# A two-layer decoder trunk on one core: the gate products of the S5 mixer in float32

## The chip, the cores and the metric

The kernel runs on one core of a Trainium2 chip. The time is that of the device for one execution, in microseconds; several executions of the same kernel are taken and the median is given. The engines are named as in the profile: PE (TensorE, matrix products), PEld (its weight loads), DVE (VectorE), ACT (ScalarE), POOL (GpSimd) and SP (SyncE, here only a queue that issues transfers).

## The reference

```python
h = x                                               # (1, 256, 1024), float32
for layer in range(2):
    h = h + 0.5 * swiglu(rms_norm(h), w_gate, w_up, w_down)       # width 2816
    hn = rms_norm(h)
    h = h + (s5_mixer(hn, ...) if layer == 0 else moba_mixer(hn, ...))
    h = h + 0.5 * swiglu(rms_norm(h), w_gate, w_up, w_down)

def s5_mixer(h, w_in, ..., d_skip, w_glu, w_out):
    u = h @ w_in                                    # 256 x 1024
    # 64 groups of 16 channels, 64 complex states each:
    #   state = lambda * state + B u;   y = Re(C state) + d_skip * u
    g = gelu(y)
    g = g * sigmoid(g @ w_glu)                      # the gate, 1024 x 1024
    return g @ w_out
```

All arrays are float32.

## The kernel before, in words

The six stages run one after the other: f00 (the first SwiGLU), s5, f01, f10, moba, f11. All order on the engines is written out by hand: the program's order is each engine's order, and no scheduler changes it.

**Split products.** A float32 matrix is taken apart into a high part, rounded to fewer bits (the type fp32r in the profile), and a low part, the difference. A product is then three: high by high, high by low, low by high, added up in PSUM. `Stream` does this for the weights. A unit is 256 rows (or two times 128 by 512) of a weight, 1 MB, loaded from HBM into one of three raw buffers in the order of the list `units`; a raw buffer is loaded again when its unit has been freed. `split` makes the high part of half a unit on ACT (L84, or L90 where a gain is multiplied in) and the low part on DVE (L85, L91) and puts both in one of nine slots; after the second half the unit is free. `pump` splits the next half in the list if it has been loaded and a slot is free, and does nothing otherwise; `get` splits until the wanted half is there; `release` gives a slot back. So a call of `pump` splits whatever comes next in the list, ahead of its use.

**S5.** Four input products (`w_in`, lines L397 to L399, two column halves by two row halves) give U, by way of ACT (L976) and a transposition on DVE (L977). The state is computed in eight blocks b of 128 channels, with tables that were prepared during f00, went to HBM and come back as TA, TE and TB, three buffers each:

- `t1(b)`: the scan input on PE (L986), from TA and U, into a PSUM bank. Blocks 0 to 3 need the first column half of U, blocks 4 to 7 the second.
- `rot(b)`: on DVE a rotation and two scans (L1005 to L1011), with decays rh from ACT (L995); on POOL the rotation back (L1015 to L1018), which gives hr. `t1rot(b)` is both, `t1ld` and `rot_ld` are the two with the next loads.
- `y_out(b)`: the output on PE (L1044), from TB, U and hr; gelu on ACT (L1048); a transposition by 32 on DVE into gs (L1051).
- `g_tr(b)`: two transposes on PE (L1060); the result goes as high part (L1062, ACT), low part (L1063, DVE) and in float32 (L1064, ACT, into gf) to SBUF.
- `glu(b)`: the gate products of the block (L1077 to L1079), eight output tiles by three products of 256 columns, into four PSUM banks.

The loop runs `y_out(b)`, `glu(b - 3)`, `t1rot(b + 3)`, `g_tr(b - 1)`. Four times `gate` follows: a sigmoid on ACT, the product with gf on DVE, and its high and low part, both on DVE (L1092, L1093). Then come the output products `so` (L397 to L399) in four blocks; the last two are done in `boundary` together with the entry of f01.

**The front.** While the first weights arrive, `busy` lets PE multiply ones; `quarter` transposes a quarter of x and multiplies the gain in (L1339 on ACT, L1340 on DVE); the first products are L471. `tables` is a generator that prepares the S5 tables during f00, a step at a time: `fill`, called beside the products, advances it by one yield. Its scalar part runs on POOL (L686 to L692), with one reciprocal on DVE (L774).

Of the kernel before, what the change touches and what calls it, by code (L numbers as in the profile page):

```python
# [10 lines left out]
F32 = mybir.dt.float32  # L11
F32R = mybir.dt.float32r
AF = mybir.ActivationFunctionType
OP = mybir.AluOpType
# [11 lines left out]
TWO_PI = 2.0 * math.pi  # L26
MAGIC = 12582912.0

XO = {'f00': 124, 's5': 124, 'g': 8, 'f01': 80, 'f10': 8, 'moba': 124, 'f11': 8}
AO = (68, 68, 68, 68)  # L30
OO = 68

# [3 lines left out]
class Stream:  # L36


    def __init__(self, nc, units, raw_pool, hl_pool):
        self.nc, self.units, self.rp, self.hp = nc, units, raw_pool, hl_pool  # L40
        self.raw = {}
        self.issued = {}
        self.clock = lambda: 0.0
        self.aged = True
        self.freed = set()
        self.nd = 0
        self.halves = []
        self.first = {}
        for u in range(len(units)):
            self.first[u] = len(self.halves)  # L50
            self.halves += [(u, 0), (u, 1)]
        self.hl = {}
        self.slots = list(range(HB - 1))
        self.ns = 0
        self.dmas()
# [63 lines left out]
def trunk_kernel(ctx: ExitStack, tc, x, ffn_norm, ffn_w_gate, ffn_w_up, ffn_w_down, mix_norm,  # L119
# [3 lines left out]
    nc = tc.nc  # L123
# [4 lines left out]
    xp = ctx.enter_context(tc.tile_pool(name="xt", bufs=1))  # L128
# [5 lines left out]
    def psM():  # L134
        return pp.tile([128, 512], F32, name="pM", tag="M", bufs=2)

    def psR():
        return pp.tile([128, 512], F32, name="pR", tag="R", bufs=2)

    def psA(i):  # L140
        return pp.tile([128, 512], F32, name=f"pA{i}", tag=f"A{i}", bufs=1)

    mm = nc.tensor.matmul


    NB = 8
# [6 lines left out]
    units = []  # L153
    where = {}
    GAIN = {"f00": None, "f01": 8, "f10": 16, "f11": 24, "s5": 32, "moba": 40}

    def add(key, load, gains=None):

        where[key] = len(units)
        units.append((key, load, gains))  # L160

    ahead = []

# [13 lines left out]
    def ld_rows(w, r0):  # L177
        def f(t):
            nc.sync.dma_start(t.rearrange("p (k c) -> p k c", c=1024),
                              w[r0:r0 + 256, :].rearrange("(k p) c -> p k c", p=128))  # L180
        return f
# [16 lines left out]
    def s5_units():  # L198
        for nh in range(2):
            for a in range(2):  # L200
                add(("win", nh, a), ld_cols(s5_w_in[0], a * 512, nh * 512), GAIN["s5"] + 4 * a)
        for b in range(4):
            add(("glu", b), ld_rows(s5_w_glu[0], b * 256))
        for b in range(4):
            add(("so", b), ld_rows(s5_w_out[0], b * 256))

    QKV = [("k", 0), ("q", 0), ("k", 1), ("q", 1), ("v", 0), ("v", 1)]
    QOFF = {"q": 0, "k": 1024, "v": 2048}
# [106 lines left out]
    def home(pool, ph):  # L315

        xa = pool.tile([128, 4224], F32R, name="xa")
        v = xa[:, XO[ph]:XO[ph] + 4096].rearrange("p (i k c) -> p i k c", i=2, c=256)
        return v[:, 0], v[:, 1]
# [298 lines left out]
    def tables(tp):  # L618
# [3 lines left out]
        def T(name, *shape):  # L622
            return tp.tile([128] + list(shape), F32, name=name)
# [147 lines left out]
            pt(lt[:, 1, :, o], u2[:, 1], w2[:, 0], OP.add)  # L771

        cfr, cfi = T("cfr", 32), T("cfi", 32)
        V.reciprocal(rden, den)  # L774
        pts(y, lr, -1.0, OP.add)
        pt(e0, y, ar, OP.mult)
# [180 lines left out]

    def s5(nxt, entry):
        V, P = nc.vector, nc.gpsimd
        HALVES = (slice(0, 64), slice(64, 128))  # L960
        wstack = ExitStack()
        wp = wstack.enter_context(tc.tile_pool(name="s5", bufs=1))
# [8 lines left out]
        def w_in(nh, t, hooks, pumps=(1, 5)):  # L971
            uA, uB = where["win", nh, 0], where["win", nh, 1]
            ps = psM()
            product(ps, t, uA, uB, hooks, pumps)
            us = wp.tile([128, 512], F32, name="us", bufs=1)
            nc.scalar.activation(us, ps, AF.Identity, scale=Rr[t])  # L976
            V.transpose(U[:, nh * 16:(nh + 1) * 16, t, :], us.rearrange("p (q c) -> p q c", c=32))  # L977

        def t1(b):
            tv = TA.pop(b).rearrange("p (i q c) -> p i q c", i=2, c=128)  # L980
            ps = psA(b) if b < 4 else psM()
            for i in range(2):
                for q in range(4):
                    c = i * 256 + q * 64
                    for r in HALVES:
                        mm(ps[r, c:c + 64], tv[:, i, q, r], U[:, 4 * b + q, :, :], start=True, stop=True)  # L986
            S[b] = ps
# [33 lines left out]
        def t1ld(b):  # L1021
            t1(b)
            if b + 3 < NB:
                ld_a(b + 3)

        def t1rot(b):
            t1ld(b)
            rot_ld(b)

        def rot_ld(b):  # L1030
            rot(b)
            if 0 < b < NB - 2:
                ld_e(b + 2)

        def y_out(b):
            tb = TB.pop(b)
            v2 = tb[:, 0:1024].rearrange("p (i q c) -> p i q c", i=2, c=128)
            v3 = tb[:, 1024:1536].rearrange("p (q c) -> p q c", c=128)
            ps = psR()
            hr = H.pop(b)  # L1040
            for q in range(4):
                for i, (v, z) in enumerate(((v3[:, q], U[:, 4 * b + q]), (v2[:, 0, q], hr[:, 0, q]), (v2[:, 1, q], hr[:, 1, q]))):
                    for r in HALVES:
                        mm(ps[r, q * 64:(q + 1) * 64], v[:, r], z, start=i == 0, stop=i == 2)  # L1044
            if b + 3 < NB:
                ld_b(b + 3)
            yg = wp.tile([128, 4, 2, 32], F32, name="yg", bufs=1)
            nc.scalar.activation(yg.rearrange("p q t c -> p (q t c)"), ps[:, 0:256], AF.Gelu_apprx_tanh)  # L1048
            gs = wp.tile([128, 2, 4, 32], F32, name="gs", bufs=2)
            for t in range(2):  # L1050
                V.transpose(gs[:, t], yg[:, :, t, :])  # L1051
            GS[b] = gs

        def g_tr(b):
            ps = psR()
            gs = GS.pop(b)
            if b == 0:
                GT["h"], GT["l"] = home(xp, "g")
            for t in range(2):
                nc.tensor.transpose(ps[:, t * 128:(t + 1) * 128], gs[:, t].rearrange("p q c -> p (q c)"),  # L1060
                                    ident)
            nc.scalar.activation(GT["h"][:, b, :], ps[:, 0:256], AF.Copy)  # L1062
            V.tensor_tensor(GT["l"][:, b, :], ps[:, 0:256], GT["h"][:, b, :].bitcast(F32), op=OP.subtract)  # L1063
            nc.scalar.activation(gf[b // 2][:, b % 2, :], ps[:, 0:256], AF.Copy)  # L1064

        def glu(b, os=range(8)):

            u = where["glu", b // 2]
            if b == 0:
                for i in range(4):  # L1070
                    acc[i] = psA(i)
            gh, gl = GT["h"][:, b, :], GT["l"][:, b, :]
            wh, wl = st.get(u, b % 2)
            for o in os:
                d = acc[o // 2][:, (o % 2) * 256:(o % 2) * 256 + 256]
                c = slice(o * 128, o * 128 + 128)
                mm(d, wh[:, c], gh, start=b == 0 and o % 2 == 0, stop=False, skip_group_check=True)  # L1077
                mm(d, wh[:, c], gl, start=False, stop=False, skip_group_check=True)
                mm(d, wl[:, c], gh, start=False, stop=b == NB - 1, skip_group_check=True)  # L1079
                if o == 7:  # L1080
                    st.release(u, b % 2)
                if o == 3 and b < 5 or o == 7 and b in (3, 4) or o == 5 and b == 4:
                    st.pump()

        def gate(i):

            sg = fp.tile([128, 2, 256], F32, name="sg", tag="gr", bufs=2)
            nc.scalar.activation(sg, acc[i].rearrange("p (a c) -> p a c", a=2), AF.Sigmoid)
            g = gf[i]
            V.tensor_tensor(g, g, sg, op=OP.mult)  # L1090
            gh, gl = (GT[p][:, 2 * i:2 * i + 2, :] for p in "hl")
            V.tensor_copy(gh, g)  # L1092
            V.tensor_tensor(gl, g, gh.bitcast(F32), op=OP.subtract)  # L1093

        def so(b, t, n, last=False):
# [6 lines left out]
        w_in(0, 0, entry_hooks("s5") if entry else {})  # L1102
        w_in(0, 1, {})
        w_in(1, 0, {3: [lambda: t1rot(0)], 5: [lambda: t1rot(1)]})
        w_in(1, 1, {1: [lambda: t1rot(2)], 4: [lambda: t1ld(3)]}, ())
        rot_ld(3)
        y_out(0)
        y_out(1)
        t1ld(4)
        g_tr(0)  # L1110
        rot_ld(4)
        y_out(2)
        g_tr(1)
        t1rot(5)
        for b in range(3, NB):
            y_out(b)
            glu(b - 3)
            if b + 3 < NB:
                t1rot(b + 3)
            g_tr(b - 1)  # L1120
        wstack.close()
        lstack.close()
        XP[0] = xstack.enter_context(tc.tile_pool(name="xt2", bufs=1))
        g_tr(7)
        st.pump(2)
        warm(AF.Sigmoid)
        glu(5)
        for i in range(4):
            glu(6, (2 * i, 2 * i + 1))
            glu(7, (2 * i, 2 * i + 1))  # L1130
# [211 lines left out]
    def busy(n):  # L1342

        ps = psR()
        for _ in range(n):
            mm(ps[:, 0:128], ones, ones, start=True, stop=True)
# [29 lines left out]
    busy(7)  # L1376
    quarter(0, gains)
    busy(3)
    st.pump()
    next(tab, None)  # L1380
    square(0, 0)
# [68 lines left out]
```

## Time and profile before

| | |
|---|---|
| median of 3 runs | 1001.4 us (1000.97 to 1001.5) |
| the profiled execution | 1001.1 us |
| its span | 999.3 us |
| PE busy | 979.9 us of it |
| DVE busy | 703.3 us |
| ACT busy | 575.7 us |
| POOL busy | 167.2 us |

The profile shows one execution. A timeline's line gives the start in us from the span's start, the length, engine, line, operation, output <- inputs, the forms, and in brackets the idle time of the engine before it with what ended it. A view of the stretches gives for each engine its busy time and its number of instructions, then the clock granted to PE as a share of full speed, the busy share of the transfer engines and GB/s. A view of the waits gives the waiting instruction, what it waited for, the sum in us, how often, and the longest. The front lies in the first 30 us, S5 from about 224 us to about 333 us.

### The profile page before, as it was taken

The page shows a single profiled execution, that of the slowest core. Times are in us where ns is not written, and L with a number is a line of the kernel's source. Part 1 is how long each engine was busy: PE and PEld are TensorE (multiplying, and loading weights), DVE is VectorE, ACT ScalarE, POOL GpSimd, SP SyncE. Part 2 cuts the span into 40 slices and gives each one's busy share as a digit, 9 for nine tenths or more (in the row PEclk, how much of TensorE's full clock was granted, in tenths as well). Part 3 has the DMA queues.
Part 4 walks back from the last instruction along what each step waited for, and adds up shares of the span by engine and source line. Part 5 has one row for each costly group of instructions (what it writes and reads, how often), then busy time and mean ns, then how long its engine had stood idle before and what let it go on. Part 6 is the DMA issues. An engine that isn't in the chain of part 4 may idle for free.

```text
span 999.3 us, 17186 instructions
## 1 busy us (share of the span) xinstructions
PE 979.9 (98%) x6700; PEld 870.9 (87%) x6700; DVE 703.3 (70%) x1147; ACT 575.7 (58%) x1045; POOL 167.2 (17%) x330
## 2 busy tenths in 40 slices
PE   8999999999889999999999999999999999999998
PEld 6778888888778999999999999998888899999997
DVE  4799676858978776666657766665689667766662
ACT  6647778744245655555455655553798656555541
POOL 4881222113740100000010000000441010000000
PEclk9999999999999999999999999999999999999999
DMA  8978776886846566555527665655354446756531
GB/s 234 275 259 257 263 250 214 277 325 217 283 139 214 179 199 219 184 192 185 189 81 227 215 209 175 206 172 171 128 169 148 154 162 212 241 180 210 170 128 42
DMA packets 138081, 198.67 MB, mean 199 GB/s; under 512 B 16320, under 2 KB 109584, under 8 KB 137744
## 3 DMA queue, kind: packets, MB, share of 16 engines
q1 hardware_dynamic: 133808, 184.32, 57.1%
q0 software_dynamic: 3616, 12.66, 3.2%
q8 instruction: 52, 0.85, 0.4%
q10 hardware_dynamic: 576, 0.61, 0.3%
q14 instruction: 29, 0.24, 0.1%
HBM read 183.89 MB, written 13.66 MB: 198 GB/s over the span
## 4 chain that ended last, share of the span: by engine, by line
PE 86%; DVE 7%; POOL 3%; issue 2%; ACT 2%; DMA 1%; SPq 0%; ACTq 0%; DVEq 0%
PE pM L552 12%; PE pM L551 12%; PE pM L553 12%; PE pA L397 9%; PE pA L399 9%; PE pA L398 9%; PE pM L397 5%; PE pM L398 5%; PE pM L399 5%; DVE wlo L85 2%; DVE zo L1011 1%; POOL sc L686 1%; PE pR L331 1%; PE pR L880 1%; ACT whi L84 1%
## 5 line engine op out<-in xcount | busy, mean ns | idle before, releaser
L551 PE MATMUL pM<-xa,whi 128*128 128x256 f32 x1056 | 295.7, 280 | 0.0
L552 PE MATMUL pM<-xa,whi 128*128 128x256 f32 x1056 | 294.9, 279 | 0.0
L553 PE MATMUL pM<-xa,wlo 128*128 128x256 f32 x1056 | 294.7, 279 | 0.0
L91 DVE SCALAR_TENSOR_TENSOR wlo<-raw,gT,whi 128x512 fp32r<-128x512 f32 x328 | 228.1, 747 | 71.2 <-ACT whi L90 71.0
L85 DVE TENSOR_TENSOR wlo<-raw,whi 128x1024 fp32r<-128x1024 f32 (+1 forms) x157 | 191.6, 1234 | 57.6 <-ACT whi L84 56.4
L90 ACT ACTIVATE whi<-raw,gT 128x512 fp32r<-128x512 f32 x328 | 213.6, 711 | 19.6 <-PE pA L399 14.7
L552 PEld LDWEIGHTS pM<-xa,whi 128*128 128x128 f32 x1056 | 198.5, 188 | 2.6
L551 PEld LDWEIGHTS pM<-xa,whi 128*128 128x128 f32 x1056 | 198.5, 188 | 2.3
L553 PEld LDWEIGHTS pM<-xa,wlo 128*128 128x128 f32 x1056 | 198.5, 188 | 0.0
L84 ACT ACTIVATE whi<-raw 128x1024 fp32r<-128x1024 f32 (+1 forms) x157 | 160.9, 1049 | 28.0 <-DMA raw<-in_ffn_w_up_dram 6.4
L397 PE MATMUL pA<-whi,ah 128*128 128x512 f32 x352 | 138.8, 394 | 0.0
L398 PE MATMUL pA<-wlo,ah 128*128 128x512 f32 x352 | 137.6, 391 | 0.0
L399 PE MATMUL pA<-whi,al 128*128 128x512 f32 x352 | 137.6, 391 | 0.0
L566 ACT ACTIVATE sg<-gr 128x256 f32<-128x256 f32 x66 | 27.6, 418 | 165.8 <-DVE gr L563 165.8
L397 PE MATMUL pM<-whi,xa 128*128 128x512 f32 x288 | 119.5, 415 | 0.0
L398 PE MATMUL pM<-wlo,xa 128*128 128x512 f32 x288 | 113.1, 393 | 1.1 <-DVE wlo L85 0.8
L399 PE MATMUL pM<-whi,xa 128*128 128x512 f32 x288 | 112.7, 391 | 0.0
L346 POOL TENSOR_TENSOR ms<-ss 128x1 f32<-128x1 f32 x10 | 1.9, 193 | 472.0 <-ACT sq L343 472.0
L399 PEld LDWEIGHTS pA<-whi,al 128*128 128x128 f32 x352 | 66.1, 188 | 14.4
L397 PEld LDWEIGHTS pA<-whi,ah 128*128 128x128 f32 x352 | 66.1, 188 | 11.5
L398 PEld LDWEIGHTS pA<-wlo,ah 128*128 128x128 f32 x352 | 66.2, 188 | 11.3
L563 DVE TENSOR_TENSOR gr<-pM,rrow 128x512 f32<-128x512 f32 x66 | 45.5, 689 | 40.6 <-PE pM L553 40.5
(262 smaller groups left out, 1234.9 us busy)
## 6 DMA issues: line engine op xcount, KB each, us to landing
raw<-in_ffn_w_down_dram SPq DMA_DIRECT2D x44, 1024.0 KB, 5.8
raw<-in_ffn_w_gate_dram SPq DMA_DIRECT2D x80, 512.0 KB, 4.0
raw<-in_ffn_w_up_dram SPq DMA_DIRECT2D x80, 512.0 KB, 5.1
raw<-in_moba_w_qkv_dram SPq DMA_DIRECT2D x12, 1024.0 KB, 5.2
TB<-dB SPq DMA_DIRECT2D x8, 768.0 KB, 6.1
raw<-in_ffn_w_gate_dram SPq DMA_DIRECT2D x16, 256.0 KB, 4.4
raw<-in_ffn_w_up_dram SPq DMA_DIRECT2D x16, 256.0 KB, 4.8
dB<-tt POOLq DMA_DIRECT2D x16, 256.0 KB, 5.3
```

The source lines that it names most:

```text
L84: nc.scalar.activation(hi[:, c], r[:, c], AF.Copy)
L85: nc.vector.tensor_tensor(lo[:, c], r[:, c], hi[:, c].bitcast(F32), op=OP.subtract)
L90: nc.scalar.activation(hi[:, c], r[:, c], AF.Identity, scale=g)
L91: nc.vector.scalar_tensor_tensor(lo[:, c], r[:, c], g, hi[:, c].bitcast(F32), op0=OP.mult, op1=OP.subtract)
L397: mm(o, xh, wh, start=start, stop=False)
L398: mm(o, xh, wl, start=False, stop=False)
L399: mm(o, xl, wh, start=False, stop=stop)
L551: mm(o, a, xh, start=k == 0 and i == 0, stop=False, skip_group_check=True)
L552: mm(o, a, xl, start=False, stop=False, skip_group_check=True)
L553: mm(o, b, xh, start=False, stop=k == 7, skip_group_check=True)
L563: V.tensor_tensor(gr, ps.rearrange("p (i c) -> p i c", i=2), Rr["row"][:, None, :].to_broadcast([128, 2, 256]), op=OP.mult)
L566: nc.scalar.activation(sg, gr[:, 0, :], AF.Silu)
```

## The change

- The gate weights are no longer split. `glu(b)` multiplies the raw float32 weight with the float32 gf: one product for each output tile in place of three. `Stream` leaves such units (`whole`) out of the list of halves; the raw buffer is freed after the second block of its unit. `g_tr` no longer makes high and low parts.
- The order of the units: gate weights and output weights alternate (gate 0, gate 1, output 0, gate 2, output 1, gate 3, output 2, output 3), where before the four gate units came first.
- The output of block 0 and the scan input of block 3 move into the last input product; the loop is now `g_tr(b)`, `y_out(b + 1)`, `t1rot(b + 4)`, `glu(b)`. `t1(3)` uses another PSUM bank. The calls of `pump` stand at other places.
- In `gate` the high part is made by ACT instead of DVE. The tile that holds the gate's parts starts at 124 in its buffer instead of 8.
- In the front, eleven products whose result nobody reads follow the ones of `busy`; in `tables`, five yields stand ahead of the reciprocal.

```diff
-XO = {'f00': 124, 's5': 124, 'g': 8, 'f01': 80, 'f10': 8, 'moba': 124, 'f11': 8}
+XO = {'f00': 124, 's5': 124, 'g': 124, 'f01': 80, 'f10': 8, 'moba': 124, 'f11': 8}
...
-            self.halves += [(u, 0), (u, 1)]
+            if not units[u][3]:
+                self.halves += [(u, 0), (u, 1)]
...
-        for b in range(4):
-            add(("glu", b), ld_rows(s5_w_glu[0], b * 256))
-        for b in range(4):
-            add(("so", b), ld_rows(s5_w_out[0], b * 256))
+        for key in (("glu", 0), ("glu", 1), ("so", 0), ("glu", 2), ("so", 1), ("glu", 3), ("so", 2), ("so", 3)):
+            w = s5_w_glu if key[0] == "glu" else s5_w_out
+            add(key, ld_rows(w[0], key[1] * 256), whole=key[0] == "glu")
...
         cfr, cfi = T("cfr", 32), T("cfi", 32)
+        for _ in range(5):
+            yield
         V.reciprocal(rden, den)
...
+        PUMPS = {2: (3,), 3: (3,), 5: (0, 4)}
...
-            ps = psA(b) if b < 4 else psM()
+            ps = psA(b) if b < 3 else psM()
...
-            if b == 0:
-                GT["h"], GT["l"] = home(xp, "g")
...
-            nc.scalar.activation(GT["h"][:, b, :], ps[:, 0:256], AF.Copy)
-            V.tensor_tensor(GT["l"][:, b, :], ps[:, 0:256], GT["h"][:, b, :].bitcast(F32), op=OP.subtract)
             nc.scalar.activation(gf[b // 2][:, b % 2, :], ps[:, 0:256], AF.Copy)
...
-            gh, gl = GT["h"][:, b, :], GT["l"][:, b, :]
-            wh, wl = st.get(u, b % 2)
+            w = st.raw[u][:, b % 2 * 1024:b % 2 * 1024 + 1024]
             for o in os:
-                d = acc[o // 2][:, (o % 2) * 256:(o % 2) * 256 + 256]
-                c = slice(o * 128, o * 128 + 128)
-                mm(d, wh[:, c], gh, start=b == 0 and o % 2 == 0, stop=False, skip_group_check=True)
-                mm(d, wh[:, c], gl, start=False, stop=False, skip_group_check=True)
-                mm(d, wl[:, c], gh, start=False, stop=b == NB - 1, skip_group_check=True)
-                if o == 7:
-                    st.release(u, b % 2)
-                if o == 3 and b < 5 or o == 7 and b in (3, 4) or o == 5 and b == 4:
+                mm(acc[o // 2][:, (o % 2) * 256:(o % 2) * 256 + 256], w[:, o * 128:o * 128 + 128],
+                   gf[b // 2][:, b % 2, :], start=b == 0 and o % 2 == 0, stop=b == NB - 1, skip_group_check=True)
+                if o in PUMPS.get(b, ()):
                     st.pump()
+                if o == 7 and b % 2:
+                    st.free_raw(u)
...
-            V.tensor_copy(gh, g)
+            nc.scalar.activation(gh, g, AF.Copy)
...
-        w_in(1, 1, {1: [lambda: t1rot(2)], 4: [lambda: t1ld(3)]}, ())
-        rot_ld(3)
-        y_out(0)
-        y_out(1)
-        t1ld(4)
-        g_tr(0)
-        rot_ld(4)
-        y_out(2)
-        g_tr(1)
-        t1rot(5)
-        for b in range(3, NB):
-            y_out(b)
-            glu(b - 3)
-            if b + 3 < NB:
-                t1rot(b + 3)
-            g_tr(b - 1)
+        w_in(1, 1, {1: [lambda: t1rot(2)], 4: [lambda: y_out(0)], 6: [lambda: t1rot(3)]}, ())
+        for b in range(6):
+            g_tr(b)
+            y_out(b + 1)
+            if b + 4 < NB:
+                t1rot(b + 4)
+            glu(b)
+        y_out(7)
+        g_tr(6)
         wstack.close()
         lstack.close()
         XP[0] = xstack.enter_context(tc.tile_pool(name="xt2", bufs=1))
         g_tr(7)
-        st.pump(2)
         warm(AF.Sigmoid)
-        glu(5)
+        GT["h"], GT["l"] = home(xp, "g")
         for i in range(4):
             glu(6, (2 * i, 2 * i + 1))
             glu(7, (2 * i, 2 * i + 1))
...
     busy(3)
+    ps = psR()
+    for a in ("h",) * 4 + ("l",) * 7:
+        mm(ps[:, 0:256], X[a][:, 1, 0:128], X["h"][:, 1, :], start=True, stop=True)
     st.pump()
```

More of the change, by code (lines that the diff above doesn't have):

```diff
@@ L155, in trunk_kernel, with add @@
     GAIN = {"f00": None, "f01": 8, "f10": 16, "f11": 24, "s5": 32, "moba": 40}
-    def add(key, load, gains=None):
+    def add(key, load, gains=None, whole=False):
         where[key] = len(units)
-        units.append((key, load, gains))
+        units.append((key, load, gains, whole))
     ahead = []
```

## The prediction

> **What bounds the kernel now.** I read the page first, then the table of stretches over the S5 stage, then the waits of TensorE (PE) there, and then the timelines of PE, VectorE (DVE), ScalarE (ACT) and of SP, the queue that issues the loads. The page says that the whole is bound by PE; the stretches (start:end, length, busy PE, PEld, DVE, ACT, POOL, then clock, DMA share, GB/s) show that S5 is the exception.
>
> ```profile
> span 999.3 us, 17186 instructions
> ...
> PE 979.9 (98%) x6700; PEld 870.9 (87%) x6700; DVE 703.3 (70%) x1147; ACT 575.7 (58%) x1045; POOL 167.2 (17%) x330
> ...
> 255.00:265.00 10.00, 5.86 (x116) 5.05 (x118) 9.40 (x19) 2.15 (x6) 7.64 (x8) 0.83 0.85 316
> ...
> 275.00:285.00 10.00, 6.70 (x112) 5.99 (x110) 8.80 (x17) 2.18 (x5) 6.33 (x6) 1.00 0.36 112
> ...
> 295.00:305.00 10.00, 9.86 (x81) 9.33 (x79) 7.25 (x8) 7.57 (x13) 0.00 (x0) 1.00 0.74 266
> ```
>
> In two of these stretches PE is idle for 4.1 and 3.3 us while DVE is busy for 9.4 and 8.8. The waits name the places, and one line of PE's timeline marks the end of the stage's gate products, the point to which I compare: the first output product starts at 305.66.
>
> ```profile
> PE pR L1060 <- ACT gf L1064: 4.0, 2, 2.1
> PE pR L1060 <- DVE gs L1051: 4.0, 1, 4.0
> ...
> 305.66 0.48 PE L397 MATMUL pA<-whi,xa 128*128 128x512 f32 x1 [0.53 <-DVE xa L1092]
> ```
>
> So the gate stage offers at most 8.5 us of idle PE, and what the long gap costs in clock, to a change that relieves DVE and ACT. From 305.66 on PE has no wait until the next stage is under way, so a shift of that point goes through to the end.
>
> **PE's part of a gate block.** One round of the loop before is a scan input (L986), the transposes of the gate input (L1060), the output of a block (L1044) and a gate block (24 products, first L1077, until the next L986):
>
> ```profile
> 269.54 1.15 PE L986 MATMUL pM<-U,TA 128*64 128x64 f32 x32
> 270.63 0.44 PE L1060 MATMUL pR<-cst,gs 128*128 128x128 f32 x2
> 270.99 0.34 PE L1044 MATMUL pR<-U,TB 128*64 128x64 f32 x4
> ...
> 272.54 0.38 PE L1077 MATMUL pA<-xa,whi 128*128 128x256 f32 x1
> ...
> 275.54 1.15 PE L986 MATMUL pM<-U,TA 128*64 128x64 f32 x32
> ```
>
> That gives 1.09, 0.36, 1.55 and 3.00 us. The change replaces the three split products for each output tile by one in float32. The nearest row is attention's float32 product of the same shape, 256 columns, recorded as two passes:
>
> ```profile
> 771.92 0.59 PE L1251 MATMUL pR<-pT,vs 128*128 128x256 f32 x2
> 772.35 0.39 PE L1252 MATMUL pR<-pT,vs 128*128 128x128 f32 x2
> ```
>
> From one start to the next it takes 0.43 us. Eight of them are 3.44, with the start of a block some 3.55: 0.55 us more than 3.00, over eight blocks 4.4 us more work on PE. [...]
>
> **What is taken from DVE and ACT.** Eight splits (L84 and L85) of the gate weights go, eight subtractions (L1063) and eight roundings to high parts (L1062), and four casts (L1092) change from DVE to ACT. Most of it stood in the rounds after 260 us; there it was what held PE at L1060, and there all of the 4.0 us of the first of the two waits can go.
>
> **What it does not take away, and what it delays.** The start of the gate phase is set by DVE, and no split of a gate weight stands in that stretch that isn't replaced. The built order shows it: where the first two halves of gate weights were split, DVE and ACT now split two halves of the first output weights, at the same places, one ahead of the first scan and one ahead of the third. Those were loaded third and not first.
>
> ```profile
> 234.52 0.37 SPq L179 DMA_DIRECT2D raw<-in_s_w_glu_dram  x1
> ...
> DMA to landing us min/median/max: 4.9/5.4/13.9
> ...
> 236.45 1.05 ACT L84 ACTIVATE whi<-raw 128x1024 fp32r<-128x1024 f32 x1
> ```
>
> The first row is the third of these loads. It waits for its buffer until the last input weights are split, and nothing of the change makes that earlier. With the shortest landing, 4.9 us, the data are there at 239.4. ACT, which began its half at 236.45, now begins 3.0 us later; on ACT the decays of the first two scans (L995) are queued behind it, and on DVE the subtraction L85 is queued ahead of the first scan:
>
> ```profile
> 237.53 1.22 DVE L85 TENSOR_TENSOR wlo<-raw,whi 128x1024 fp32r<-128x1024 f32 x1 [0.23 <-ACT whi L84]
> 238.71 0.06 DVE L994 MEMSET rh<- 128x4 f32 x1
> ...
> 242.18 0.06 DVE L994 MEMSET rh<- 128x4 f32 x1
> ...
> 254.15 0.68 DVE L977 STREAM_TRANSPOSE U<-us 128x512 f32<-128x512 f32 x1
> ...
> 254.78 0.67 DVE L1006 TENSOR_TENSOR wv<-pA,TE 128x512 f32<-128x512 f32 x1
> ...
> 259.68 0.47 DVE L1051 STREAM_TRANSPOSE gs<-yg 128x128 f32<-128x128 f32 x2
> ```
>
> So the first scan starts at about 241.75, not 238.71. The new order on DVE from there: scans 0 to 2 with the second split and one transposition of U (15.4 us, 238.71 to 254.15), the transposition gs of block 0 (0.42), scan 3 (4.90, 254.78 to 259.68), and only then the last transposition of U (0.68), which stood before scan 3 and on which the scan input of block 4 depends. It is ready at 263.2. PE meets that scan input before its first gate block, since "one block sooner" puts it ahead of gate block 0; with semaphores PE goes on at 263.3. Until then it has less work than time. The output of block 0, now inside the last input product, waits there for POOL's part of scan 0; the rest of that product and the scan input of block 3 stand behind it on PE and still finish before gs of block 0 at 257.65. Transposes and the output of block 1 (0.36 and 1.55) then end near 259.6, and the gap up to 263.3 is some 3.7 us.
>
> **From there PE sets the time.** DVE needs 4.9 us for a scan and 0.5 for a transposition in a round, PE 0.36 + 1.55 + 1.09 + 3.55 = 6.55. PE's sum: scan input 1.1, gate block 0 3.55, three whole rounds 19.65, two rounds without a scan input 10.9, the output of block 7 1.55, then two sets of transposes with the wait for the last gelu and transposition between them (rows below: 0.38 and 0.51, with semaphores about 0.75 us not covered by the first set) 1.46, and the last two gate blocks 7.0. Sum 45.2.
>
> ```profile
> 278.61 0.38 ACT L1048 ACTIVATE yg<-pR 128x256 f32<-128x256 f32 x1
> ...
> 279.02 0.51 DVE L1051 STREAM_TRANSPOSE gs<-yg 128x128 f32<-128x128 f32 x2 [0.73 <-ACT yg L1048]
> ```
>
> So 263.3 + 45.2 = 308.5, and the output products start at 308.6, 2.9 us later than 305.66, with the wait of 0.53 there gone (each gate now has 1.7 us of PE beside it). The loads of the later weights are issued after blocks 1, 3 and 5, two or more rounds ahead of their use; they are hidden by PE's own rounds of 6.55 us, and would cost up to one landing, 4.9 us, if that cover were gone.
>
> **The clock.** After the gap of 4.0 us before, the clock fell to half:
>
> ```profile
> 260.70 0.48 PE L1044 MATMUL pR<-U,TB 128*64 128x64 f32 x4 [0.16 <-ACT yg L1048]
> ...
> 263.46 0.67 PE L1060 MATMUL pR<-cst,gs 128*128 128x128 f32 x2
> ...
> 261.00:262.00 1.00, 1.00 (x24) 1.00 (x22) 1.00 (x5) 0.47 (x2) 1.00 (x2) 0.50 1.06 412
> ```
>
> One output took 2.76 us instead of 1.55; with the transposes around it the fall cost about 1.5 us, which 305.66 already holds. The new gap of 3.7 us ends just as dense products begin. I take the same price, 1.5, since the gap is nearest to that one; the other end is nothing. Stage S5: +4.4 us (+2.9 with a full clock).
>
> **Position of the gate tile.** Moved from offset 8 to 124. The output products (L399, one third of 96) show 399 ns from offset 8; the input products, from 124, show 391:
>
> ```profile
> L399 PE MATMUL pM<-whi,xa 128*128 128x512 f32 x288 | 112.7, 391 | 0.0
> ...
> L399 PE MATMUL pA<-whi,xa 128*128 128x512 f32 x32 | 12.8, 399 | 0.0
> ```
>
> At most 96 x 8 ns = 0.8 us are won; what runs beside them differs as well, so I take 0.3, and 0 as the other end.
>
> **The front.** Eleven products of nothing fill PE's wait of 1.88 us; the five yields move the reciprocal (L774) behind two splits on DVE.
>
> ```profile
> 5.82 0.87 DVE L1340 SCALAR_TENSOR_TENSOR xa<-pA,gT,xa 128x256 fp32r<-128x256 f32 x2 [0.54 <-ACT xa L1339]
> 7.97 2.17 PE L471 MATMUL pA<-whi,xa 128*128 128x512 f32 x4 [1.88 <-ACT whi L84]
> 10.93 0.31 PE L662 MATMUL pR<-cst,scn 32*128 32x32 f32 x1
> 11.79 1.16 PE L471 MATMUL pA<-whi,xa 128*128 128x512 f32 x4
> 13.25 0.60 PE L1332 MATMUL pA<-cst,xn 128*128 128x128 f32 x4
> ...
> 23.89 0.35 DVE L774 RECIPROCAL rden<-den 128x32 f32<-128x32 f32 x1 [2.35 <-POOL den L686]
> 25.38 0.50 PE L398 MATMUL pM<-wlo,xa 128*128 128x512 f32 x1 [0.81 <-DVE wlo L85]
> 46.02 0.23 DVE L701 COPY e<-c 128x16 f32<-128x16 f32 x1 [3.86 <-POOL c L692]
> 53.05 0.44 PE L495 MATMUL pR<-cst,act 128*128 128x128 f32 x2 [1.33 <-DVE act L482]
> ```
>
> The first six real products took 2.96 us (7.97 to 10.93), the next six 1.46: the first group ran at half clock. The eleven read what DVE leaves at 6.69; at 0.125 us each they end before 7.97 and keep the clock up: 1.5 us at most. At half clock they would take twice as long and push the first product back by about 0.8. The reciprocal gives back up to 0.8 of the wait at 25.38. But the stall at 46.02 hangs on POOL's chain, which starts from the last squares on ACT; by ACT's and DVE's order in between these move forward by about 1.0, and PE's wait at 53.05 takes the rest. I take -1.2, between +0.8 and -2.3. [...]
>
> **Sum.** +4.4 - 0.3 - 1.2 = +2.9 us. The profiled execution took 1001.1, 0.3 under the median of 1001.4; added to the median this gives 1004.3. About 0.2%, 2 us, is what a measurement of this kernel can tell from no change: slower begins at 1003.4, faster ends at 999.4.
>
> **The rivals.**
> - Full clock after the new gap: +2.9 instead of +4.4, total +1.4, 1002.8. For it: gaps of 2.1 us passed without a fall; against it: 3.7 is nearer to 4.0. Chance 0.17.
> - The output weights are not late (their load finds its buffer 3 us sooner): S5 +1.4, total -0.1, 1001.3. Against it: the order of the loads is unchanged. Chance 0.10.
> - Faster: DVE reaches the last transposition of U sooner, because scans 1 to 3 don't collide with POOL and each take the 3.47 us of scan 0 (238.71 to 242.18). That saves 5.1 us, the gap is gone with its fall of the clock, and the output products start at 303.5: -2.2 - 1.5 = -3.7, 997.7. It decides if PE goes on before 259.9. Against it: POOL has the same work at the same places. Chance 0.13, with all that I misjudge to this side.
> [...]
> - The products of nothing buy nothing, because the clock stays up without them or falls in spite of them: the front gives 0.2, 1005.3. Chance 0.07.
>
> **How the numbers follow.** The forecast, 1004.3, has 0.47. Slower: 0.47, 0.06, 0.07 and 0.05 of the first rival, 0.65. Within 0.2%: 0.12 of the first rival and 0.10, 0.22. Faster: 0.13. The range leaves out the faster case and a little above the dearest, 999.8 to 1008.0; the forecast's own range, with the ends of front, clock and position, is 1002 to 1006.5.
>
> **What would show it.** Right: L84's successor on ACT waiting about 3 us for a load near 236, the first scan on DVE 3 us later, a PE gap of over 3 us ahead of the scan input of block 4 with half clock behind it, no PE wait in the rounds after it, a gate block of about 3.55 us, and six first products of 1.5 us near 8 us. Wrong: gate blocks of 3.0 or of 4.0 us, waits for gs or for a raw weight in the rounds, or the output products starting before 305.

## The result, and the profile after

| | before | after |
|---|---|---|
| median | 1000.9 us (14 runs) | 1002.9 us (14 runs, 1001.8 to 1006.3) |
| ratio to before | | 1.002 [1.0011, 1.0028] |
| the profiled execution | 1001.1 us | 1003.1 us |
| its span | 999.3 us | 1001.4 us |

The change makes the kernel 2.0 us slower; 2.9 were predicted. The page of the changed kernel (its first line and that of the busy times) shows 53 matmuls fewer in the records and 5.4 us more of busy PE, while DVE has lost 18.6 us and ACT 6.8. The lines behind the edits have moved (L84 is L85, L986 is L989, L1044 is L1047, L1060 is L1061, L1077 is L1073, L1332 is L1319). The brackets behind a ratio are its 95% interval.

```profile
span 1001.4 us, 17050 instructions
...
PE 985.3 (98%) x6647; PEld 873.9 (87%) x6647; DVE 684.7 (68%) x1127; ACT 568.9 (57%) x1033; POOL 163.2 (16%) x330
```

The waits of PE over S5 in the changed kernel (what waits, for whom, sum, times, longest): 6.4 us where there were 8.7, and at other places. No wait is left at the output products.

```profile
PE pR L1061 <- DVE gs L1054: 2.7, 2, 2.2
PE pM L989 <- DVE U L980: 2.5, 1, 2.5
PE pR L1047 <- POOL hr L1020: 0.7, 1, 0.7
PE pR L1047 <- POOL hr L1021: 0.5, 1, 0.5
```

The timelines of ACT, DVE and PE in the changed kernel give the chain that was forecast. An output weight comes late (ACT waits 3.18 us for it, DVE 3.52), the first scan starts at 241.23, the last transposition of U (L980) ends behind scan 3 at 262.59, and the scan input of block 4 (L989) follows at 262.64:

```profile
238.97 1.06 ACT L85 ACTIVATE whi<-raw 128x1024 fp32r<-128x1024 f32 x1 [3.18 <-DMA raw<-in_s_w_out_dram]
...
240.06 1.23 DVE L86 TENSOR_TENSOR wlo<-raw,whi 128x1024 fp32r<-128x1024 f32 x1 [3.52 <-ACT whi L85]
241.23 0.68 DVE L1009 TENSOR_TENSOR wv<-pA,TE 128x512 f32<-128x512 f32 x1
...
260.18 1.81 DVE L1014 TENSOR_TENSOR_SCAN zo<-rh,zi 128x260 f32<-128x260 f32 x2
261.91 0.68 DVE L980 STREAM_TRANSPOSE U<-us 128x512 f32<-128x512 f32 x1
...
262.64 1.39 PE L989 MATMUL pM<-U,TA 128*64 128x64 f32 x32 [2.48 <-DVE U L980]
263.97 5.10 PE L1073 MATMUL pA<-gf,raw 128*128 128x256 f32 x16
268.90 0.38 PE L1061 MATMUL pR<-cst,gs 128*128 128x128 f32 x2
...
270.66 1.10 PE L989 MATMUL pM<-U,TA 128*64 128x64 f32 x32
271.69 3.72 PE L1073 MATMUL pA<-gf,raw 128*128 128x256 f32 x16
275.25 0.38 PE L1061 MATMUL pR<-cst,gs 128*128 128x128 f32 x2
...
308.47 0.58 PE L397 MATMUL pA<-whi,xa 128*128 128x512 f32 x1
```

A gate block takes 3.56 us from one start to the next (271.69 to 275.25), the first one 4.93 (263.97 to 268.90), since the clock fell: the stretches of the changed kernel show 0.66 and 0.84 over 255 to 265 us. The output products start at 308.47 instead of 305.66.

The front is shorter by 0.73 us at the second input product of f00 (L495, 53.05 before), where it still waits for what hangs on POOL's chain:

```profile
52.32 0.44 PE L495 MATMUL pR<-cst,act 128*128 128x128 f32 x2 [2.04 <-DVE act L482]
```

From L495 to the first output product it is 252.61 us before (305.66 - 53.05) and 256.15 after: S5 costs +3.54. This distance leaves the front out, so it is given for the kernels below.

### The profile page after: what moved, and what is told of

The parts are those of the page before. It is cut to its first block, busy times and chain, and to the rows that moved or that the text cites. A ratio compares the mean times of both kernels' runs of the same rounds, so it can differ in the third digit from the quotient of the medians.

```text
span 1001.4 us, 17050 instructions
## 1 busy us (share of the span) xinstructions
PE 985.3 (98%) x6647; PEld 873.9 (87%) x6647; DVE 684.7 (68%) x1127; ACT 568.9 (57%) x1033; POOL 163.2 (16%) x330
## 4 chain that ended last, share of the span: by engine, by line
PE 87%; DVE 5%; POOL 3%; issue 2%; ACT 1%; DMA 1%; SPq 0%; ACTq 0%; DVEq 0%; POOLq 0%
PE pM L552 12%; PE pM L551 12%; PE pM L553 12%; PE pA L397 9%; PE pA L399 9%; PE pA L398 9%; PE pM L397 5%; PE pM L398 5%; PE pM L399 5%; PE pA L1073 3%; POOL sc L686 1%; DVE wlo L86 1%; PE pR L1047 1%; PE pR L331 1%; PE pR L882 1%
## 5 line engine op out<-in xcount | busy, mean ns | idle before, releaser
L86 DVE TENSOR_TENSOR wlo<-raw,whi 128x1024 fp32r<-128x1024 f32 (+1 forms) x149 | 180.1, 1222 | 58.6 <-ACT whi L85 57.4
L85 ACT ACTIVATE whi<-raw 128x1024 fp32r<-128x1024 f32 (+1 forms) x149 | 152.8, 1048 | 31.0 <-PE pA L399 6.7
L399 PE MATMUL pA<-whi,al 128*128 128x512 f32 x352 | 137.6, 391 | 0.0
L399 PE MATMUL pM<-whi,xa 128*128 128x512 f32 x288 | 112.7, 391 | 0.0
L399 PEld LDWEIGHTS pA<-whi,al 128*128 128x128 f32 x352 | 66.1, 188 | 14.3
```

Source lines behind the costliest of these rows:

```text
L85: nc.scalar.activation(hi[:, c], r[:, c], AF.Copy)
L86: nc.vector.tensor_tensor(lo[:, c], r[:, c], hi[:, c].bitcast(F32), op=OP.subtract)
L399: mm(o, xl, wh, start=False, stop=stop)
```

## The experiments

**Two placements, apart and together.** The theory: the loss doesn't lie in the float32 product but in two placements, an output weight that is split ahead of the first scan although its load is late, and the last transposition of U behind scan 3. The first kernel splits nothing during the third input product.

```diff
-        w_in(1, 0, {3: [lambda: t1rot(0)], 5: [lambda: t1rot(1)]})
+        w_in(1, 0, {3: [lambda: t1rot(0)], 5: [lambda: t1rot(1)]}, ())
```

> The two pumps of the third input product are taken out, so that the first output weights are split where the later pumps stand (gate blocks 2 and 3), not ahead of the scans. Theory (the late load and the splits ahead of the scans set the start of the gate phase): the first scan on VectorE starts about 3 us sooner, the scan input of block 4 about 4.2 us sooner (near 258.4 instead of 262.6), the output products near 303 to 304 instead of 308.5; 4 to 5.5 us off the changed kernel's 1002.9, about 998. Rival (the dearer float32 products alone make the loss, the start is covered): no change, 1002.9, and the time won at the start comes back as a wait in the rounds, now that VectorE splits there.

Measured: 999.54 us, 0.9989 [0.998, 0.9999] of before; from L495 to the first output product 252.44 us. The output products start later than expected, at 304.95. The timeline of DVE has the first scan 2.8 us sooner, and that of PE shows where it went:

```profile
238.43 0.69 DVE L1009 TENSOR_TENSOR wv<-pA,TE 128x512 f32<-128x512 f32 x1 [1.61 <-PE pA L989]
...
258.28 0.68 DVE L980 STREAM_TRANSPOSE U<-us 128x512 f32<-128x512 f32 x1
...
259.06 1.15 PE L989 MATMUL pM<-U,TA 128*64 128x64 f32 x32 [3.90 <-issue]
260.15 5.41 PE L1073 MATMUL pA<-gf,raw 128*128 128x256 f32 x16
...
304.95 0.58 PE L397 MATMUL pA<-whi,xa 128*128 128x512 f32 x1
```

The wait for gs of 2.2 us is gone, but the one for U grows to 3.90, and the first gate block is still at half clock (0.50 in every stretch from 260.5 to 263.5 us). (The view names no releaser for it; the transposition of U ends at 258.96, 0.1 ahead of L989.) The second kernel keeps the early splits and moves only the scan behind the transposition of U:

```diff
-        w_in(1, 1, {1: ..., 4: [lambda: y_out(0)], 6: [lambda: t1rot(3)]}, ())
+        w_in(1, 1, {1: ..., 4: [lambda: y_out(0)], 6: [lambda: t1ld(3)]}, ())
+        rot_ld(3)
```

> Scan 3 is issued behind the last input product instead of inside it, so that the last transposition of U comes ahead of scan 3 on VectorE. Theory (that transposition, queued behind scan 3, holds the scan input of block 4): that scan input starts when the output of block 1 is done, near 259.5 to 260 instead of 262.6, without the 2.5 us wait of PE and with less time at half clock; 2.5 to 4 us off, about 999.6. Rival (PE's sum from there is not what sets the end, VectorE's scans are): scan 3 ends 0.7 later and everything after it too, 1002.9 to 1003.6.

Measured: 998.27 us, 0.9974 [0.9963, 0.9985]; the distance is 250.38 us. PE's timeline has the gap ahead of gs, and no other of over 0.6 us; the scan input follows without a wait, and the gate block runs at full clock (1.00 over 255 to 260 and over 260 to 265 us). (The profile is that of the shortest execution, 997.06 us. Three of the seven, 997.06 to 997.94, show a mean granted clock of 1.000; the other four, 998.27 to 998.66, show 0.998.)

```profile
256.37 0.43 PE L1061 MATMUL pR<-cst,gs 128*128 128x128 f32 x2 [2.25 <-DVE gs L1054]
...
258.18 1.10 PE L989 MATMUL pM<-U,TA 128*64 128x64 f32 x32
259.21 3.72 PE L1073 MATMUL pA<-gf,raw 128*128 128x256 f32 x16
262.77 0.38 PE L1061 MATMUL pR<-cst,gs 128*128 128x128 f32 x2
```

The third kernel has both edits.

> Both edits of the two runs before. Theory: PE goes from the input products to the last gate block with under 1 us of waits and no fall of the clock; scan input of block 4 near 254.7, output products near 299, about 9.5 us off: 993.5. That is less than the sum of PE's idle time and half clock in the changed kernel's stage, some 8 us of waits and 3 of clock. Rival (VectorE becomes the bound of the rounds: a scan 4.9, a transposition 0.5 and a split 1.2 to 2.0 are 6.6 to 7.4 in two rounds against PE's 6.35): 1 to 2 us of waits for gs come back, 995.

Measured: 993.37 us (993.04 to 993.61), 0.9928 [0.9911, 0.9944]: 7.4 us under before, 9.5 under the changed kernel, and the fastest here. The distance is 246.60 us, 6.0 under before. Its waits of PE over S5 are one line, and its timeline has the scan input of block 4 at 254.58, 8 us sooner than in the changed kernel, with the output products at 298.74:

```profile
PE pR L1061 <- DVE gs L1054: 0.5, 1, 0.5
```

```profile
252.77 0.43 PE L1061 MATMUL pR<-cst,gs 128*128 128x128 f32 x2
...
254.58 1.10 PE L989 MATMUL pM<-U,TA 128*64 128x64 f32 x32
255.61 3.72 PE L1073 MATMUL pA<-gf,raw 128*128 128x256 f32 x16
259.17 0.38 PE L1061 MATMUL pR<-cst,gs 128*128 128x128 f32 x2
...
298.74 0.58 PE L397 MATMUL pA<-whi,xa 128*128 128x512 f32 x1
```

Apart the edits bring 3.35 and 4.6 us, together 9.5: alone, each leaves one of the two gaps standing.

**The order of the units.** The changed kernel with the gate weights first and the output weights behind them, as before. Then no output weight has been loaded when the first scan is due.

```diff
-        for key in (("glu", 0), ("glu", 1), ("so", 0), ("glu", 2), ("so", 1), ("glu", 3), ("so", 2), ("so", 3)):
+        for key in [("glu", b) for b in range(4)] + [("so", b) for b in range(4)]:
```

> The changed kernel with the weights of the gate first and then those of the output, as before the change. Theory: nothing can be split ahead of the scans, since the output weights aren't loaded yet; the same start as in the run without the early splits, about 998, and the splits move behind the gates, where PE has 11 us of output products before it needs the third unit: 998 to 999. Rival (the alternation is what keeps PE supplied at the output products): the output products wait for splits by 2 us or more, 1000 or above.

Measured: 999.64 us, 0.9989 [0.9979, 0.9998], the time of the first kernel and a little above the 998 to 999 expected, with the same wait of 3.90 us at L989. (The distance is 253.63 us, 1.2 longer than there: in this profile the clock stayed at half for 6.83 us around the end of that wait, in the first kernel's for 3.41.) The two edits have nothing in common but that the early split goes, and they give the same time: what the interleaved order costs, it costs through that split.

**The float32 product alone.** The kernel before, with float32 gate products from unsplit weights; order, units, front and tile position are those of before. The splits of the gate weights and of the gate input go with the old product, and so do the calls of `pump` in the gate blocks. The edit is shown in part.

```diff
...
-                mm(d, wh[:, c], gh, start=b == 0 and o % 2 == 0, stop=False, skip_group_check=True)
-                mm(d, wh[:, c], gl, start=False, stop=False, skip_group_check=True)
-                mm(d, wl[:, c], gh, start=False, stop=b == NB - 1, skip_group_check=True)
+                mm(acc[o // 2][:, (o % 2) * 256:(o % 2) * 256 + 256], w[:, o * 128:o * 128 + 128],
+                   gf[b // 2][:, b % 2, :], start=b == 0 and o % 2 == 0, stop=b == NB - 1, skip_group_check=True)
...
```

> The kernel before with the float32 gate products from unsplit weights alone: its order of blocks, its order of units, its front and its gate casts are kept; of the gate input only the float32 copy is made. No output weight is split ahead of the first scan, since the next units in the list are the gate's, which are not split. Theory (the loss came from the early splits of output weights and from the last transposition of U behind scan 3, not from the float32 products): DVE is relieved, the first gap of 8 us in all shrinks, the output products start at 303 to 304 and the time is about 999.5, 1.5 under before. Rival (the loss is the dearer product, 0.55 us for each of eight blocks): 3 to 4 us slower than before, 1004 to 1005.

Measured: 998.55 us, 0.998 [0.997, 0.9989]; the distance is 250.78 us, 1.83 under before. The dearer product pays, with the splits that it saves: of the waits of PE over S5, 8.7 us before, one is left, and that buys more than the 0.56 us a block cost. (What the missing calls of `pump` bring by themselves was not measured.)

```profile
PE pR L1059 <- DVE gs L1052: 3.4, 1, 3.4
```

**The position of the gate tile alone,** on the kernel before.

```diff
-XO = {'f00': 124, 's5': 124, 'g': 8, 'f01': 80, ...}
+XO = {'f00': 124, 's5': 124, 'g': 124, 'f01': 80, ...}
```

> The kernel before with the position of the gate tile alone moved from 8 to 124. Theory: the pitch of the output products falls from 0.2333 to 0.2265 us as in the changed kernel, over 96 products 0.65 us: 1000.3. Rival: the pitch follows from what runs beside the products and not from the position, then it stays 0.233 and the time that of before.

Measured: 1000.4 us against 1000.9, 0.9992 [0.9983, 1.0002]. The time alone can't tell it from no change. The group by form hardly can: the output products (L399) show 394 ns, where before shows 399 and the changed kernel 390, but the kernel with the float32 product alone, which has offset 8, shows 395.

```profile
L399 PE MATMUL pA<-whi,xa 128*128 128x512 f32 x32 | 12.6, 394 | 0.0
```

From the first to the last of the 96 it is 23.30 us before (305.66 to 328.96), 22.80 here and 22.66 in the changed kernel. Offset 8 gives 23.21 to 23.30 in three profiles, 124 between 22.66 and 22.88 in ten. So 0.5 of the 0.64 us follows the position; the other 0.14 is no more than the profiles at 124 differ among themselves.

**The front.** First on the kernel before, with its two edits alone (eleven products of nothing, five yields), then taken out of the changed kernel one by one and together, and together out of the fastest kernel. The edit in each is one or both of:

```diff
+    ps = psR()
+    for a in ("h",) * 4 + ("l",) * 7:
+        mm(ps[:, 0:256], X[a][:, 1, 0:128], X["h"][:, 1, :], start=True, stop=True)
...
+        for _ in range(5):
+            yield
```

> The kernel before with the front's part of the change alone (eleven products of nothing, five yields). Theory: in the changed kernel the front came out 0.73 us shorter at the point where the stage behind it starts (the stall of DVE at L701 started at 45.26 instead of 46.02), so 1000.2, 0.7 under before; the first six products take 1.9 us instead of 2.96, and the wait at 25.38 is gone. Rival: the front is hidden anyway, the time is that of before within 0.2; other rival: the products of nothing cost what they hold up, +0.3 or more.

Measured: 1000.21 us, 0.7 under before, 0.9995 [0.9985, 1.0004], which does not exclude no change.

> The changed kernel without the eleven products of nothing; the five yields stay. Theory: the first six real products run at half clock again and take 3.0 us instead of 1.9; of these 1.1 us most is given back at the quarter behind them and at the stall on POOL's chain at L701, which moves by 0.3 to 0.5: 1003.3, 0.3 to 0.5 over the changed kernel. Rival: the yields bring the whole 0.73 and the products of nothing are hidden: the time of the changed kernel. Other rival: they are what brings it: +0.7 to 1.0.

Measured: 1002.84 us, the time of the changed kernel. The first six products take 2.69 us (3.0 expected) where the changed kernel has 1.90, and nothing of it arrives in the median. The changed kernel's own timeline shows where most of it goes. PE begins the second six products 1.77 us sooner than before (10.02 against 11.79), and then waits for DVE at the transposes of the next quarter of x, so that the six products behind these begin only 0.22 sooner (13.38 against 13.60):

```profile
12.79 0.83 PE L1319 MATMUL pA<-cst,xn 128*128 128x128 f32 x4 [1.15 <-DVE xa L1327]
```

Nor do the products of nothing always have a fall to prevent. In the six profiles without them PE waits for the first weight between 0.58 and 1.88 us. The first six products run wholly or in part at half clock in three of these (waits of 1.64 to 1.88; 2.61 to 2.96 us) and at full clock in the other three (waits of 0.58 to 0.97; 1.88 and 1.89 us).

> The changed kernel with the front of before: neither the eleven products of nothing nor the five yields. In the profiles so far the start of L495 (the second input product of f00, behind the stall on POOL's chain) lies at 53.05, 51.84 and 52.02 with the front of before, and between 51.59 and 52.51 in six profiles with the new front. Theory 1 (the 0.73 of the front seen between the first two profiles is mostly scatter of one execution, from when the first weights land): the time of the changed kernel within 0.3, 1002.6 to 1003.2. Theory 2 (the front brings what the first two profiles showed): 1003.6, 0.7 over the changed kernel.

Measured: 1004.47 us (1003.47 to 1004.96), 1.6 over the changed kernel: above both theories. Theory 1 falls, and the 0.7 of theory 2 is too small for this median; but the intervals of the two ratios, 1.0035 [1.0023, 1.0047] here and 1.002 [1.0011, 1.0028] for the changed kernel, overlap. The distance is 256.08 us, as in the changed kernel.

> The changed kernel without the five yields; the products of nothing stay. Theory 1 (the front is scatter): 1002.6 to 1003.2. Theory 2 (the yields bring what there is, since the run without the products of nothing came out at 1002.84, as the changed kernel): 1003.3 to 1003.6, with PE's wait of 0.8 for the subtraction near 25 us back in the trace.

Measured: 1004.47 us (1003.14 to 1005.4), as much as without both and above what theory 2 gave. PE's wait of 0.8 us near 25 us is back:

```profile
25.49 0.50 PE L398 MATMUL pM<-wlo,xa 128*128 128x512 f32 x1 [0.82 <-DVE wlo L86]
```

The profile, of the longest execution (1005.4 us), also has S5 itself 1.25 us longer than the changed kernel (257.40 against 256.15), though nothing was changed there. The clock stays up in the first gap and falls in the second, for 6.83 us instead of 3.41, so that the scan input and most of the first gate block run at half clock:

```profile
263.48 1.97 PE L987 MATMUL pM<-U,TA 128*64 128x64 f32 x32 [3.86 <-DVE U L978]
265.39 5.85 PE L1071 MATMUL pA<-gf,raw 128*128 128x256 f32 x16
271.07 0.38 PE L1059 MATMUL pR<-cst,gs 128*128 128x128 f32 x2
```

> The fastest kernel so far (no early splits, last transposition of U before scan 3) with the front of before. Theory 1: 993.1 to 993.7, the time of that kernel (993.37). Theory 2: 994.0 to 994.2.

Measured: 994.58 us, 1.2 over the fastest kernel, more than theory 2 gave; the distance is 246.67 us, as there. So the front brings 0.7, 1.6 and 1.2 us by the medians of three pairs of kernels, and in each pair the intervals leave its size open. The medians put all of it on the yields. But executions differ in their mean granted clock, in the changed kernel from 0.993 to 0.998. Among those at 0.998 the changed kernel has 1001.82 to 1002.62 us (five), without the products of nothing 1002.55 to 1002.87 (three), without the yields 1003.14 and with the front of before 1003.47 (one each). That puts some 0.8 us on the yields and a little on the products of nothing, on few executions. One profile can't show it either: with the front of before, L495 starts at 53.05, 51.84, 52.02, 53.66 and 52.88 in five profiles, with the new one between 51.59 and 52.51 in six, with the yields alone at 52.80 and with the products of nothing alone at 53.24. How the front's gain divides between the two was not settled.

## Why the prediction was right

By its own steps, the prediction against the changed kernel's profile:

| step | predicted | measured |
|---|---|---|
| late output weight: ACT's start, first scan | 3.0 us later, each | 2.52 later, 238.97 against 236.45, and 2.52; with the 0.73 of the front 3.25 |
| scan input of block 4 | 263.3 | 262.64; with the 0.73 of the front 263.37 |
| gate block | 3.55 | 3.56 |
| round | 6.55 | 6.35 |
| PE's sum at full clock | 45.2 | 44.16 |
| cold clock | 1.5 | 1.67 |
| S5 | +4.4 | +3.54 |
| position | -0.3 | -0.64, of which 0.5 shown as its own |
| front | -1.2 | -0.73 in this pair of profiles; 0.7 to 1.6 by medians |
| sum | +2.9 | +2.17 by these terms, +2.1 by the spans, +2.0 by the medians |

The mechanism is the one forecast: late load, scan, U behind scan 3, gap, half clock, then a stage bound by PE. Of the signs that were named, two did not come as worded: the gap ahead of the scan input of block 4 is 2.48 us and not over 3, and the first six products take 1.90 us and not 1.5.

That the number fits is partly luck. The direction is shown, since the interval of the ratio lies above 1; but the prediction drew its line for slower at 2 us, and with 1.95 the result lies at the edge of the case "within 0.2%", which had 0.22. The forecast of 1004.3 was 1.4 us above the measured 1002.9: 0.5 of that lies in the median of before (1001.4 over 3 runs, 1000.9 over 14), 0.9 in the terms. As a number, 1002.9 is what the first rival gave (1002.8, full clock behind the gap); the fall of the clock in the trace rules that rival out, the time alone would not.

One term was mis-sized, PE's sum, by 1.04 us. The three whole rounds took 19.05 us instead of 19.65, the last two gate blocks 6.73 instead of 7.0 and the transposes ahead of them 1.31 instead of 1.46; the two rounds without a scan input came out as forecast, 10.93 against 10.9. The round was put together from pieces of the loop before: 0.36 for the transposes, 1.55 for an output, 1.09 for a scan input. There these pieces stood in another order. In the new loop the same rows are 0.31 (275.25 to 275.56), 1.45 with a scan input behind the output, and 1.03 with a gate block behind the scan input (270.66 to 271.69): 0.2 us a round. It is the neighbour that goes with the difference and not the stops: where a gate block follows the output, as in the loop before, the output takes 1.55 us again, in a stretch of the new loop in which PE never stops:

```profile
288.26 0.34 PE L1047 MATMUL pR<-U,TB 128*64 128x64 f32 x4
...
289.81 3.72 PE L1073 MATMUL pA<-gf,raw 128*128 128x256 f32 x16
```

With 44.16 us for this sum, S5 would have been forecast at +3.4.

The cold clock came out close for a reason that the prediction did not have. Two gaps, of 2.20 and 2.48 us, each brought half clock, not one of 3.7. The first spell lies where PE waits for U anyway and shortened the second gap, which is 3.86 us in the kernel without the yields, where that spell is missing; nothing was lost by it; the second cost the 1.67 (4.93 - 3.56 on the gate block, and 1.33 - 1.03 on the scan input). In the profile of the kernel without the yields, with the same order in S5, it is 3.0 us (5.68 and 1.91 for the two). So 1.5 was right for this execution, not for the order of work.

Of the front, the step that failed is the products of nothing. Their 1.5 us at most were the larger part of the estimate. The first products did keep the full clock (1.00 over 6 to 10 us) and took 1.06 us less (1.90 against 2.96), but the prediction had no wait for DVE at the next quarter of x behind them, 1.15 us in the trace, and the median shows no gain. What the front brings seems to come mostly from the yields, for which 0.8 at most had been given. The total was near, its parts were not.

Of the rivals, the late load that isn't late is refuted by the rows above. The upper end of the range, 1008.0, the chance of 0.06 and the sign of 4.0 us a block belong to a dearer float32 product; no run shows such a price. The block took 3.56 us, 0.445 for each of its eight products, 3.6 of the old ones at 0.125 (24 of them in 3.00 us). What either of the two records of a float32 product costs by itself, no run here shows.

The faster rival named the right lever: PE goes on before 259.9 in the four kernels with the new order in which one of the two placements, or both, is undone (259.06, 258.18, 254.58, and 258.15 with the units in order), and all four are faster than before. But S5 by itself is clearly shorter than before (252.61) only in the two with U ahead of scan 3, 250.38 and 246.60; with 252.44 and 253.63 the other two owe their gain to the front and the gate tile. And it needed a change of order, not a quicker scan. (The rival's saving is mis-added: scans 1 to 3 took 5.54, 4.66 and 4.90 us, which is 4.7 and not 5.1 over three of 3.47.)

## What to carry to other kernels

An engine's queue is a place for each step: a pump that splits "whatever comes next" changes its meaning when the list changes, and here that put a weight that had not arrived ahead of the first scan. When a change moves work off a busy engine and still loses, look for the one step on that engine that the next stage waits for, and move it to the head: three lines turned 2.0 us lost into 7.4 us won. And price a new loop from pieces that have the same neighbours there: the same output took 1.45 us ahead of a scan input and 1.55 ahead of a gate block.

## What the runs showed of the hardware

The fall of the clock is not decided by the length of a gap alone. In the changed kernel the gap ahead of gs, 2.20 us, brought half clock; in the kernel without the yields the same gap, 2.20 us, and in the kernel with U before scan 3 one of 2.25, did not (1.00 from 255 to 260 us in both). The stretches of a tenth of a us in the changed kernel (start:end, length, busy PE, PEld, DVE, ACT, POOL, then the granted clock) show where it changes, and the last row is the stretch of 3.41 us ahead of the first change:

```profile
256.50:256.60 0.10, 0.00 (x0) 0.00 (x0) 0.10 (x2) 0.00 (x0) 0.01 (x1) 0.77 1.11 430
...
259.90:260.00 0.10, 0.10 (x7) 0.10 (x4) 0.10 (x1) 0.00 (x0) 0.10 (x2) 0.67 0.00 0
...
263.30:263.40 0.10, 0.10 (x11) 0.10 (x8) 0.00 (x0) 0.00 (x0) 0.10 (x2) 0.90 0.44 184
...
266.70:266.80 0.10, 0.10 (x2) 0.10 (x1) 0.10 (x2) 0.00 (x0) 0.00 (x0) 0.54 0.45 175
...
253.15:256.56 3.41, 1.45 (x6) 0.83 (x5) 3.41 (x5) 0.69 (x1) 2.08 (x3) 1.00 0.47 136
```

Where a stretch holds a change, its clock gives the place: 0.77 over 256.50 to 256.60 means full clock for 0.054 us and half for the rest. The changes lie at 256.55, 259.97, 263.38 and 266.79, each 3.41 us behind the last. In the kernel before, the clock fell at 7.97 (0.84 over 7.90 to 8.00) and at 260.56 (0.78 over 260.50 to 260.60), and was full again at 11.38 (0.62 over 11.00 to 11.50) and at 263.97 (0.53 over 263.50 to 264.00), 3.41 us behind each fall. In the changed kernel PE was busy for 1.45 of the 3.41 us that end at 256.56, where the clock fell.

What decides whether a gap of some 2 us is paid at half clock was not shown; the same order of work on PE came out either way. The price of a longer gap varies as well: behind the same wait of 3.90 us at L989 half clock cost 1.7 us in the kernel without the early splits and 2.9 with the units in order. It shows in the times of one and the same kernel too: with the units in order, four executions at a mean clock of 0.998 took 998.74 to 999.23 us and four at 0.996 took 1000.12 to 1000.92. A difference of 1 us between two kernels is thus read with the granted clock of their executions beside it.
